# A hybrid decoder block: two segments of 256 tokens in place of segments of 128 and 384

## The chip, the cores and the metric

The kernel runs on one core of a Trainium2 chip. It is one program on that core's five engines: TensorE (PE in the profile, with its weight loads shown apart as PEld), VectorE (DVE), ScalarE (ACT), GpSimd (POOL) and SyncE (SP), which here only issues DMAs. The metric is the device time of one launch in microseconds (us); lower is better. The time before is 1791.47 us, the median of two runs (1790.25 and 1792.68).

## The reference

The input is 512 tokens of 1024 channels in float32. What is computed, cut to what matters:

```python
xn   = rmsnorm(h, mix_norm_w)
proj = xn @ w_in              # pool groups | q,k,v | z | beta | decay | gates
y_a  = pool_mixer(xa, ...) @ w_pool_up         # causal windows 2, 4, 8, 16
y_b  = deltanet_branch(qkv, z, ...) @ w_dn_up  # 8 heads, conv of 4, chunked scan
h    = h + (sigmoid(gate_a) * y_a + sigmoid(gate_b) * y_b) @ w_mix_out
h    = h + peer_ffn(rmsnorm(h, ffn_norm_w), ...)
out  = rmsnorm(h, final_norm_w)

def peer_ffn(x, w_query, keys_1, keys_2, expert_down, expert_up):
    # per token and head: top 16 of 128 keys on either side, top 16 of the
    # 256 sums, softmax: 8 * 16 = 128 of 16384 experts with a gate each
    act = gelu(x . expert_down[e])
    return sum over e of gate[e] * act * expert_up[e]
```

The convolution, the pools and the scan run causally over the tokens. The last layer, the experts (peer_ffn), has 16384 rows of 1024 floats in each of its two tables.

## The kernel before

**Blocks and segments.** The 512 tokens are four blocks of 128. The front of the block, from the first normalization to the choice of the experts, is written as `segment(t0, T)`: for T tokens from t0 it loads each weight matrix once, tile by tile (0.5 MB per tile, tag `wraw`, five buffers), and multiplies all T tokens with it. `SEGMENTS` (L59) says which segments there are. Before, the first holds block 0 (128 tokens) and the second blocks 1, 2 and 3 (384 tokens). The state of the scan and the last few tokens of the convolution and of the pools are handed from one segment to the next.

**Two ways to multiply.** A segment of fewer than 256 tokens is exact: its 60 tiles of `win` and `wdn` (52 and 8) are multiplied in plain float32. From 256 tokens on the weights are split: ScalarE writes the high part of each half tile (`whi`), VectorE the rest (`wlo`), and three products of high and low parts replace the exact one, with activations split in the same way (`xwide`). `wpu`, `wmo` and `wq` are never split.

```python
exact = T < 256                                                     # L718
def wload(ap, n, exact=False):                                      # L642
    ...
    for q in range(2):
        hi, lo = whi([P, 512], F32R), wlo([P, 512], F32R)
        split(raw[:, q * 512:(q + 1) * 512], (hi, lo))
```

**Two ways to do the experts.** Blocks 0 and 1 are gathered. `select` (L958) finds the 128 experts of each of the block's tokens, and `retrieve` (L1030) fetches for each of the 128 slots one row per token from the table `down`, has VectorE take its dot product (`rows<-rows,xbuf`), applies the gelu and the gate in groups of 16, then fetches the row of `up` and has VectorE add it to the token (`hbuf<-rows,keep,hbuf`). That is 256 gathers of 0.5 MB per block, 512 in all, issued by GpSimd into four buffers, tag `rows`. Blocks 2 and 3 (the last TB = 256 tokens) are dense: `dense` (L1062) goes over the whole tables, 128 tiles of each, computes all activations and multiplies them with gates that are zero for experts not chosen. The first 28 activation tiles (`PLAIN`) are plain float32 and the others split. `gates_of_experts` builds the gates on VectorE, ScalarE and TensorE.

**The tag keep.** The small tiles of a gathered block, its indices, gates, `act` and `co`, each take one of the six units of the tag `keep` (L533), and so does the gate tile of a dense block between its `select` and its transposition.

**What sets the order.** All instructions are first recorded, then a planner (`Order.schedule`) puts them into one fixed order per engine. Among the instructions that are ready by its own costs it takes the one with the smallest virtual time: 0 for the first segment, 10 for the second, 149 for a gather, from 150 on for the dense experts (`VTS`, `FETCH`, `MOVE`); a gathered block's `select` in a segment that also has dense blocks is put at 120 (`LATE`). On the chip each engine then runs its list strictly in that order, so an instruction that waits holds up all that stand behind it on its engine. Every instruction of the profile has line 495, the one that emits the plan; groups are told apart by tile names.

Of the kernel before, what the change touches and what calls it, by code (L numbers as in the profile page):

```python
# [55 lines left out]
PARTVT = 10.0  # L56
LATE = 120.0
PLAIN = RUN
SEGMENTS = ((0, 128), (128, 384))  # L59
TB = 256  # L60
TMAX = 384

# [451 lines left out]
def block_kernel(ctx: ExitStack, tc: tile.TileContext, x, win, wbd, poolw, wpu, wdn, wmo, wq, down, up, downt,  # L514
# [819 lines left out]

    for k, (t0, T) in enumerate(SEGMENTS):
        nc.vt = VTS[k]
# [56 lines left out]
```

## Time and profile before

| | |
|---|---|
| median of the runs | 1791.47 us |
| profiled execution, device time | 1788.57 us |
| its span, first to last instruction | 1786.8 us |
| busy in that span | TensorE 94%, VectorE 86%, ScalarE 52%, GpSimd 42% |
| read from HBM | 505 MB, 284 GB/s over the span |
| mean granted TensorE clock | 0.977 of full speed |

The profile is one execution. A busy share is a mean over the whole span, in which stages with different limits follow one another: the first segment (to about 240 us), the second with the gathers of block 0 beside it (to about 925 us), and the dense experts with the rest of the gathers (to the end). The device time lies 1.8 us over the span, and the median another 2.9 us over that.

### The profile page before, as it was taken

How to read it: one execution, taken by the hardware profiler on the slowest of the kernel's cores; microseconds unless marked ns; L12 is line 12 of the kernel's file. 1: busy time of each engine (PE TensorE's matmuls, PEld its weight loads, DVE VectorE, ACT ScalarE, POOL GpSimd, SP SyncE). 2: the span in 40 equal slices, each digit the busy share in tenths (PEclk: the TensorE clock that was granted, in tenths of full speed). 3: DMA queues.
4: the chain of work that ended last, by engine and by line, in shares of the span. 5: the costliest groups of instructions: out<-in, count | busy, mean ns of one | idle time of the engine just before them, and what ended most of it. 6: DMA issues, size and time to landing. Idle time of an engine off the chain costs nothing.

```text
span 1786.8 us, 34168 instructions
## 1 busy us (share of the span) xinstructions
PE 1677.1 (94%) x12186; PEld 1455.6 (81%) x12186; DVE 1542.0 (86%) x3873; ACT 922.9 (52%) x2271; POOL 755.4 (42%) x598
## 2 busy tenths in 40 slices
PE   7999999899999999998999999899999999999992
PEld 7999899889899898498787765677777768988892
DVE  6622499988998788699999999999999999999996
ACT  6642248845734342221139946666667665555552
POOL 0000015555466653543328743545445534333334
PEclk9999999899999999999999999999999999999996
DMA  7437858567687899897767798889999999999996
GB/s 262 154 125 253 278 191 281 188 225 259 205 265 255 304 349 328 312 315 240 236 214 255 240 355 310 313 320 331 348 348 330 348 334 379 345 341 345 340 353 226
DMA packets 144746, 509.36 MB, mean 285 GB/s; under 512 B 16960, under 2 KB 21184, under 8 KB 144576
## 3 DMA queue, kind: packets, MB, share of 16 engines
q0 software_dynamic: 73728, 268.47, 43.6%
q1 hardware_dynamic: 70848, 238.72, 37.6%
q8 instruction: 95, 1.56, 0.3%
q14 instruction: 75, 0.61, 0.1%
HBM read 505.02 MB, written 2.10 MB: 284 GB/s over the span
## 4 chain that ended last, share of the span: by engine, by line
PE 42%; DVE 26%; issue 13%; DMA 10%; POOL 6%; ACT 3%; SPq 0%; POOLq 0%; DVEq 0%; ACTq 0%
PE bank L495 42%; DMA rows<-in_up_dram,keep 7%; DVE quad L495 5%; POOL rows L495 5%; DVE rows L495 4%; DVE scr L495 4%; DVE hbuf L495 4%; DVE wlo L495 4%; DMA rows<-in_down_dram,keep 2%; DVE sel L495 2%; ACT scr L495 1%; DVE xwide L495 1%; ACT L495 1%; ACT quad L495 1%; ACT whi L495 0%
## 5 line engine op out<-in xcount | busy, mean ns | idle before, releaser
L495 PE MATMUL bank<-xwide,whi 128*128 128x256 f32 (+1 forms) x2560 | 575.6, 310 | 1.1 <-ACT whi L495 1.0
L495 POOL DMA_INDIRECT rows<-in_up_dram,keep x256 | 366.0, 1430 | 367.5 <-DVE hbuf L495 170.9
L495 POOL DMA_INDIRECT rows<-in_down_dram,keep x256 | 318.0, 1242 | 431.2 <-DVE keep L495 282.1
L495 ACT CAST whi<-wraw 128x512 fp32r<-128x512 f32 x512 | 315.3, 619 | 294.4 <-PE bank L495 247.8
L495 PEld LDWEIGHTS bank<-xwide,whi 128*128 128x128 f32 x2560 | 432.4, 192 | 9.1 <-ACT whi L495 2.8
L495 PE MATMUL bank<-xwide,wlo 128*128 128x256 f32 (+1 forms) x1280 | 396.9, 310 | 7.1 <-DVE wlo L495 6.9
L495 DVE SCALAR_TENSOR_TENSOR hbuf<-rows,keep,hbuf 128x1024 f32<-128x1024 f32 x256 | 328.6, 1284 | 42.3 <-DMA rows<-in_up_dram,keep 41.7
L495 DVE TENSOR_TENSOR wlo<-wraw,whi 128x512 fp32r<-128x512 f32 x512 | 352.8, 704 | 13.0 <-ACT whi L495 9.4
L495 DVE CUSTOM_DVE_ANT_0 rows<-rows,xbuf 128x1024 f32<-128x1024 f32 x256 | 318.1, 1246 | 23.9 <-DMA rows<-in_down_dram,keep 22.7
L495 PEld LDWEIGHTS bank<-xwide,wlo 128*128 128x128 f32 x1280 | 245.1, 192 | 16.8 <-DVE wlo L495 12.0
L495 PE MATMUL bank<-whi,xwide 128*128 128x512 f32 x768 | 242.6, 397 | 4.1 <-ACT xwide L495 2.6
L495 PE MATMUL bank<-pair,wraw 128*128 128x128 f32 (+1 forms) x1600 | 217.8, 289 | 1.6 <-DVE xwide L495 0.8
L495 PEld LDWEIGHTS bank<-pair,wraw 128*128 128x128 f32 x1600 | 198.2, 196 | 9.2 <-DVE xwide L495 1.1
L495 PE MATMUL bank<-quad,wraw 128*128 128x256 f32 x704 | 172.1, 389 | 0.0
L495 PEld LDWEIGHTS bank<-whi,xwide 128*128 128x128 f32 x768 | 139.0, 189 | 35.1 <-ACT xwide L495 4.1
L495 PE MATMUL bank<-wlo,xwide 128*128 128x512 f32 x384 | 150.3, 394 | 9.3 <-DVE wlo L495 9.1
L495 ACT ACTIVATE scr<-c,c 128x128 bf16<-128x128 bf16 x384 | 139.6, 445 | 23.1 <-PE bank L495 23.0
L495 PEld LDWEIGHTS bank<-quad,wraw 128*128 128x128 f32 x704 | 127.2, 191 | 15.5 <-issue 0.8
L495 PE MATMUL bank<-wraw,quad 128*128 128x512 f32 x256 | 120.9, 610 | 2.0 <-DVE quad L495 2.0
L495 PEld LDWEIGHTS <-scr 128*128 128x128 bf16 x2304 | 72.3, 97 | 48.3 <-issue 27.7
L495 PEld LDWEIGHTS bank<-wlo,xwide 128*128 128x128 f32 x384 | 71.9, 188 | 30.1 <-DVE wlo L495 15.0
L495 ACT COPY quad<-bank 128x512 f32<-128x512 f32 (+2 forms) x119 | 55.4, 474 | 74.7 <-PE bank L495 62.9
(156 smaller groups left out, 2126.2 us busy)
## 6 DMA issues: line engine op xcount, KB each, us to landing
wraw<-in_downt_dram SPq DMA_DIRECT2D x128, 512.0 KB
wraw<-in_up_dram SPq DMA_DIRECT2D x128, 512.0 KB
wraw<-in_win_dram SPq DMA_DIRECT2D x104, 512.0 KB
wraw<-in_wq_dram SPq DMA_DIRECT2D x32, 512.0 KB
wraw<-in_wdn_dram SPq DMA_DIRECT2D x16, 512.0 KB
wraw<-in_wmo_dram SPq DMA_DIRECT2D x16, 512.0 KB
wraw<-in_wpu_dram SPq DMA_DIRECT2D x8, 512.0 KB
rows<-in_down_dram,keep POOLq DMA_INDIRECT x256
```

What stands on the lines that cost most here:

```text
L495: ins = getattr(getattr(self.nc, eng), meth)(*(real(a) for a in args), **{k: real(a) for k, a in kw.items()})
```

## The change

One line of numbers is changed. The first segment then holds blocks 0 and 1, both gathered, and the second blocks 2 and 3, both dense. As neither is shorter than 256 tokens, neither is exact, and all tiles of `win` and `wdn` are split in both.

```diff
-SEGMENTS = ((0, 128), (128, 384))
+SEGMENTS = ((0, 256), (256, 256))
```

The planner makes a new order from this. Two places matter below. The first is GpSimd's list. `scr<-scr` are its additions in the convolution (128x256 or 128x384) and the pools (widths a little over the segment's); `small` are small powers; `rows<-in_down_dram,keep` is a gather. Before, from the pools of the first segment on:

```order
L495 TENSOR_TENSOR scr<-scr 128x137
L495 TENSOR_TENSOR scr<-scr 128x129
L495 TENSOR_TENSOR small<-small,c_82 128x1
L495 DMA rows<-in_down_dram,keep 128x1024
L495 TENSOR_TENSOR scr<-scr 128x384
L495 DMA rows<-in_down_dram,keep 128x1024 x3
```

The same place of the list now:

```order
L495 TENSOR_TENSOR scr<-scr 128x256 x14
L495 TENSOR_TENSOR small<-small,c_82 128x4
L495 TENSOR_TENSOR scr<-scr 128x256 x2
L495 TENSOR_TENSOR small<-small,c_82 128x4
L495 TENSOR_TENSOR scr<-scr 128x256 x8
L495 TENSOR_TENSOR small<-small,c_82 128x4 x2
L495 TENSOR_TENSOR scr<-scr 128x271 x2
...
L495 TENSOR_TENSOR scr<-scr 128x257
L495 TENSOR_TENSOR small<-small,c_82 128x1 x2
L495 DMA rows<-in_down_dram,keep 128x1024 x4
```

The first gather still stands behind the whole first segment, which now has two blocks; on VectorE the choice of experts for both blocks stands ahead of the first gathered row.

The second place is VectorE's list where the dense blocks have chosen their experts and their gates are written (`keep<-sel,small`; `c_105` are the dense blocks' gates in the form that the gate building reads). `ISA rows,keep<-rows,xbuf` is the dot product with a gathered row of `down`, `ISA keep` reads its sum, `hbuf<-rows,keep,hbuf` adds a gathered row of `up`. Before:

```order
L495 RECIPROCAL small<-small 128x8
L495 ISA rows,keep<-rows,xbuf 128x1024
L495 ISA keep 128x1
...
L495 SCALAR_TENSOR_TENSOR hbuf<-rows,keep,hbuf 128x1024
L495 TENSOR_TENSOR keep<-sel,small 128x128
L495 TENSOR_TENSOR keep<-small,keep 128x16
L495 TENSOR_TENSOR keep<-sel,small 128x128
L495 CAST c_105<-sel 128x128
```

And now (left out are 11 more pairs of ISA rows ahead of the first sum, and between the x15 row and the gate 32 more pairs and 16 more sums):

```order
L495 RECIPROCAL small<-small 128x8
L495 TENSOR_TENSOR scr<-c_85,c_105 128x2x96 x2
L495 ISA rows,keep<-rows,xbuf 128x1024
L495 ISA keep 128x1
...
L495 SCALAR_TENSOR_TENSOR hbuf<-rows,keep,hbuf 128x1024
L495 TENSOR_TENSOR keep<-small,keep 128x16
L495 SCALAR_TENSOR_TENSOR hbuf<-rows,keep,hbuf 128x1024 x15
...
L495 TENSOR_TENSOR keep<-sel,small 128x128
L495 SCALAR_TENSOR_TENSOR hbuf<-rows,keep,hbuf 128x1024
L495 CAST c_105<-sel 128x128
```

In both orders the dense gates stand behind all 128 dot products and 96 or 97 of the sums of block 0, 224 gathered rows, give or take one. Before, 221 gathered rows stand ahead of the last top-16 search of the dense blocks; now 148 do, and the other 76 stand between it and the gates, with next to nothing else among them.

## Rows read from the trace of the kernel before

**Rows 1.** Page, busy time of each engine, and chain that ended last.

```profile
PE 1677.1 (94%) x12186; PEld 1455.6 (81%) x12186; DVE 1542.0 (86%) x3873; ACT 922.9 (52%) x2271; POOL 755.4 (42%) x598
...
PE 42%; DVE 26%; issue 13%; DMA 10%; POOL 6%; ACT 3%; SPq 0%; POOLq 0%; DVEq 0%; ACTq 0%
```

**Rows 2.** Windows: stretch, length, busy PE, PEld, DVE, ACT, POOL, clock, DMA share, GB/s.

```profile
0.00:240.50 240.50, 223.77 (x1854) 214.66 (x1855) 111.75 (x488) 102.71 (x284) 10.36 (x40) 0.99 0.65 219
0.00:270.00 270.00, 252.72 (x2056) 241.63 (x2057) 140.40 (x609) 118.04 (x313) 17.28 (x46) 0.99 0.63 211
...
270.00:925.00 655.00, 627.19 (x3822) 565.86 (x3821) 589.23 (x1536) 285.37 (x633) 328.57 (x262) 0.97 0.77 264
925.00:1030.00 105.00, 97.83 (x1117) 79.47 (x1116) 102.62 (x297) 92.35 (x308) 76.63 (x32) 1.00 0.77 257
1030.00:1775.00 745.00, 699.31 (x5197) 568.66 (x5195) 705.28 (x1430) 426.01 (x1017) 331.40 (x259) 0.98 0.93 336
```

**Rows 3.** Timeline: last key scores of the first segment, first gathered row, first dense gate.

```profile
240.29 0.39 PE L495 MATMUL bank<-sel,scr 128*128 128x128 f32 x2
...
270.32 1.21 DVE L495 CUSTOM_DVE_ANT_0 rows<-rows,xbuf 128x1024 f32<-128x1024 f32 x1
...
926.50 0.28 DVE L495 TENSOR_TENSOR keep<-sel,small 128x128 f32<-128x128 f32 x1
```

**Rows 4.** Windows, VectorE on tile rows alone: stretch, length, busy (instructions), clock, DMA, GB/s.

```profile
270.00:925.00 655.00, 285.75 (x224) 0.97 0.77 264
...
704.00:745.00 41.00, 21.83 (x18) 1.00 0.96 353
1758.00:1775.70 17.70, 11.58 (x10) 0.54 0.84 293
```

**Rows 5.** VectorE's waits from 270 to 925: us in total, times, longest.

```profile
DVE hbuf L495 <- DMA rows<-in_up_dram,keep: 28.8, 23, 3.1
DVE rows L495 <- DMA rows<-in_down_dram,keep: 16.8, 16, 3.0
```

**Rows 6.** Chain in order of time (start, us, what), at two runs of bare gathers.

```profile
735.96 7.46 DMA rows<-in_up_dram,keep
...
1760.96 5.26 DMA rows<-in_up_dram,keep
```

**Rows 7.** TensorE's timeline (start, us): exact tiles, split at 384, at 256.

```profile
144.10 42.55 PE L495 MATMUL bank<-pair,wraw 128*128 128x128 f32 x376
...
601.70 0.33 PE L495 MATMUL bank<-xwide,wlo 128*128 128x384 f32 x1
...
602.22 0.33 PE L495 MATMUL bank<-xwide,wlo 128*128 128x384 f32 x1
...
1552.36 0.28 PE L495 MATMUL bank<-xwide,wlo 128*128 128x256 f32 x1
...
1552.72 0.28 PE L495 MATMUL bank<-xwide,wlo 128*128 128x256 f32 x1
```

**Rows 8.** TensorE's timeline: wmo in the first segment; plain float32 at 256.

```profile
186.48 13.90 PE L495 MATMUL bank<-wraw,pair 128*128 128x512 f32 x32
...
857.84 17.86 PE L495 MATMUL bank<-quad,wraw 128*128 128x256 f32 x82
```

**Rows 9.** Groups by line and shape: the two halves of a split.

```profile
L495 DVE TENSOR_TENSOR wlo<-wraw,whi 128x512 fp32r<-128x512 f32 x512 | 352.8, 704 | 13.0 <-ACT whi L495 9.4 <-ACT scr L495 0.6
...
L495 ACT CAST whi<-wraw 128x512 fp32r<-128x512 f32 x512 | 315.3, 619 | 294.4 <-PE bank L495 247.8 <-ACT xwide L495 11.2 <-issue 6.7
```

**Rows 10.** VectorE's timeline: three low halves in a row, and what follows.

```profile
1596.70 1.89 DVE L495 TENSOR_TENSOR wlo<-wraw,whi 128x512 fp32r<-128x512 f32 x3
1598.51 1.28 DVE L495 SCALAR_TENSOR_TENSOR hbuf<-rows,keep,hbuf 128x1024 f32<-128x1024 f32 x1
```

**Rows 11.** Windows, VectorE on tile wlo alone, columns as in Rows 4.

```profile
270.00:925.00 655.00, 79.76 (x109) 0.97 0.77 264
```

## The prediction

> **What bounds the kernel now.** I read the page's busy times first: TensorE 94% and VectorE 86% of the span, and a chain that ended last with TensorE on 42% and VectorE on 26% of it [rows 1]. Neither number says which of the two a change would hit, so I went by stages with the windows [rows 2]. The reader should see four of them. Up to 270 us VectorE is busy for only 140 us and TensorE for 253: the first segment is TensorE's. From 270, when the first gathered row is used, to 925, just before the first dense gate [rows 3], TensorE has 627 of 655 us and VectorE 589. From 925 to 1030 the rest of block 0's rows and the first dense gates fill VectorE (103 of 105). From 1030 on, the gathers of block 1 and the dense tiles run side by side, with VectorE at 705 and TensorE at 699 of 745 us and the DMA engines at 0.93. So after 270 us both engines are nearly full, and the only real idle time of VectorE is the 130 us of the first stage.
>
> Two more views say what a gathered row costs. In the windows of tile rows, VectorE uses 224 of them from 270 to 925 [rows 4], 2.9 us apart, and its waits there are mostly for rows to land, 28.8 + 16.8 us [rows 5]. The rows are not always spread, though: from 704 to 745 they stand almost bare in VectorE's list, 18 of them in 41 us, 2.3 us each, though a row costs it 1.28 us (285.75 / 224); at the end, with nearly nothing else running, it is 10 in 17.7 us, 1.8 us each by the windows [rows 4]. The chain shows why: a row takes 5.3 to 7.5 us from its issue to VectorE [rows 6], and there are four buffers.
>
> **The change part by part.** I build the span from four pieces: the first gathered row, the rows beside the second segment, the bare rows ahead of the dense gates, and the rest.
>
> *TensorE's work.* An exact tile is 16 records; 376 of them take 42.55 us, 0.113 each, so 1.81 us a tile [rows 7]. A split tile is 24 matmuls: three take 0.52 us at 384 columns (4.16 us a tile) and 0.36 at 256 (2.88) [rows 7]. The 60 tiles cost 60 x (1.81 + 4.16) = 358 us before and 60 x 2 x 2.88 = 346 after. The unsplit matrices keep their total columns. TensorE gains 12 us in all, but the first segment loses: its 60 tiles go from 109 to 173 us (+64); the 256 records of wq go from 0.113 to 0.218 (17.86 / 82 [rows 8]), +27; wmo +14, its 13.90 us once more [rows 8]; wpu +7, 64 records by the same difference. The rest of the first segment (scan, transposes) is what is left of TensorE's 224 busy us up to 240 [rows 2]: 224 - 109 - 29 - 14 - 7, and less some 9 us that already belong to the second segment, about 56 us for one block, and once more for the second. Sum: +168. The last key scores, at 240 now [rows 3], move to 408. I add 15 us, as VectorE and ScalarE get two half tiles each per 2.88 us of TensorE on top of the convolution and can no longer stay ahead everywhere (bounds 0 to 40). From the last scores to the first gathered row are 30 us now [rows 3]; two blocks choose their experts in place of one, so 46 us (30 to 60). **First gathered row at about 470 us** (440 to 500), 200 later than now.
>
> *VectorE's work.* 120 more low halves: three in a row take 1598.51 - 1596.70 = 1.81 us [rows 10], so 0.60 us each, though the group shows 0.704 for one alone [rows 9]: +73 us (72 to 84). ScalarE gets 120 casts of 0.619 us, +74 us [rows 9], at nothing: it is busy for 923 of 1787 us [rows 1], and what it delays in the first segment is in the 15 us above. The other vector work has the same elements in about as many instructions, and is put at zero (-10 to +5). HBM traffic is the same, since each segment loads all weights in either case.
>
> *The rows beside the second segment.* 148 now stand ahead of the dense blocks' last search. VectorE's work until there: from 270 to 925 it has 589 us, of which 286 for rows [rows 4] and 80 for low halves [rows 11]; the other 223 were for three blocks, so 149 for two. 113 low halves at 0.73 (80 / 109) are 83, and 148 rows at 1.28 are 189: 421 us. TensorE's part is under 400 (173 + 55 + 28 + 14 + 112 for tiles, wq, wmo, wpu and scans), so VectorE decides. With waits for rows in proportion to today's (46 x 148 / 224 = 30): **450 us** (415 to 480).
>
> *The bare rows ahead of the dense gates.* 76 rows stand alone between the last search and the gates. Nothing can hide their latency, so they go at the pace of the bare run: 2.3 us each, **175 us**. The bounds are 1.8 (137 us, the run at the end, with nothing else on the DMA engines) and 2.9 (220 us, today's mean); I take the run at 704 since weights move beside it too. TensorE has 28 plain tiles to do there, 16 x 0.218 = 3.5 us each, 98 us, and then waits.
>
> The Trainium skill's page "DMA: Bandwidth & Descriptors" (section "Anatomy of one DMA — SWDGE (gpsimd) path") gives about 2.0 us plus the bytes by 436 GB/s for such a transfer, 3.2 us for 0.5 MB; the rows here take 5.3 to 7.5. By the page four buffers would turn around in about 5.4 us, 1.4 us a row, which would make the bare run some 107 us and the span about 1873; I go by the rows.
>
> *The rest.* From the gates on, both lists hold the same work, 288 rows and all the dense tiles, which take 1787 - 925 = 862 us now. The plain tiles, which TensorE now does beside the gate building, are done by then, but VectorE fills that stretch [rows 2], so I credit 15 us (0 to 40).
>
> Sum: 470 + 450 + 175 + 847 = 1942 us of span. The device time lies 1.8 us above the span and the median 2.9 above that, so **about 1945 us**, 8.6% slower. A measurement of this kernel tells about 2% from no change.
>
> **The rivals.**
> 1. *Only the work counts.* VectorE's extra 73 us come on top and the late gathers are caught up with, as other work fills the bare run: 1788 + 73 = 1860. For it: VectorE is nearly full after 270 us [rows 2]. Against it: its list is fixed and the rows stand alone there.
> 2. *Rows come as fast as four buffers allow without load.* With 1.4 to 1.8 us a row, 107 to 137 us, the span is 1875 to 1905.
> 3. *The first segment chokes.* If VectorE and ScalarE can't keep to 2.88 us a tile and the rows go at today's 2.9, then 500 + 480 + 220 + 850 = 2050.
> 4. *Not slower.* TensorE alone is the bound: it gains 12 us, VectorE's extra work falls into its 130 idle us, and the 98 us of plain tiles done during the wait come off the rest in full. With the lower bounds of the other pieces, 440 + 415 + 137 + 764 = 1756 us, and 1788 if only part of the 98 comes off. The rest is what decides: TensorE would have to be what holds it up. For it speaks 94% busy [rows 1]; against it, that VectorE is as full there [rows 2].
>
> That the change does less than it says is ruled out by the order: 512 rows, 632 low halves, and the two waits shown.
>
> **How the numbers follow.** Forecast 0.58, rival 1 0.15, rival 2 0.14, rival 3 0.08, rival 4 0.05. The range of the forecast alone, with its pieces mostly not all at one end, is 1890 to 2000. To hold 8 in 10 it takes in rival 2 and most of rival 1: 1855 to 2000. Faster by over 2% needs rival 4 at its far end, 0.01; within 2% the rest of it, 0.04; slower 0.95.
>
> **What would show it.** The first gathered row near 470 us and not before 430. VectorE under two thirds busy until then. A stretch of some 175 us, near 920 to 1095, in which GpSimd issues a row about every 2.3 us, VectorE waits for DMAs between them, and TensorE runs out of plain tiles, idles, and may be granted a lower clock. First dense gates near 1095 in place of 925, and about 850 us from there to the end. Split matmuls at 256 columns 0.12 us apart, VectorE's busy time near 1610. If the gates come on time and the end is late all the same, the pieces are wrong; if the stretch after the gates shrinks by far more than 15 us, TensorE was the bound there and rival 4 has the better mechanism.

## The result, and the profile after

The kernel after takes 1992.02 us (median of two runs, 1989.1 and 1994.94) where the kernel before took 1791.47: 1.1103 times as long, with an interval of 1.1057 to 1.1148, 200 us more. The prediction was 1945 us in a range of 1855 to 2000, so the time came out inside the range and 47 us above the forecast. The profiled execution took 1989.1 us, its span is 1987.3, and its mean granted clock is 0.929 (0.977 before).

The page of the kernel after, busy times and two of its rows of 40 slices:

```profile
PE 1704.6 (86%) x12426; PEld 1477.4 (74%) x12426; DVE 1626.9 (82%) x3978; ACT 990.7 (50%) x2414; POOL 738.7 (37%) x621
...
DVE  7656525389998987779866799999999999999996
...
PEclk9899989997999899989975599999999999999997
...
L495 DVE TENSOR_TENSOR wlo<-wraw,whi 128x512 fp32r<-128x512 f32 x632 | 435.4, 699 | 102.0 <-ACT whi L495 97.8
```

TensorE's work is nearly what it was [rows 1] and VectorE's grew by 85 us, but the span grew by 200. Two places in the slices stand out: VectorE is at two to seven tenths for its first eight slices, some 400 us (before, its idle first stage ended at 270 us [rows 2]), and at the slices of 7, 5 and 5 tenths of the clock, from 994 to 1143 us, TensorE is busy for 33 of 149 us.

The four pieces of the prediction are seen in the timeline of the kernel after, with the last key scores of the first segment, the first gathered row, and the first dense gate:

```profile
456.05 0.61 PE L495 MATMUL bank<-sel,scr 128*128 128x128 f32 x4
...
495.56 1.21 DVE L495 CUSTOM_DVE_ANT_0 rows<-rows,xbuf 128x1024 f32<-128x1024 f32 x1
...
1128.06 0.29 DVE L495 TENSOR_TENSOR keep<-sel,small 128x128 f32<-128x128 f32 x1 [0.34 <-ACT small L495]
```

In [rows 3] these stood at 240, 270 and 926. The windows of the kernel after between them, columns as in Rows 2 (975.30 is where the first of the bare rows starts):

```profile
0.00:456.50 456.50, 419.58 (x2926) 386.35 (x2926) 256.07 (x810) 232.13 (x541) 35.42 (x67) 0.96 0.36 119
0.00:495.50 495.50, 442.01 (x3062) 402.95 (x3063) 294.79 (x1028) 241.34 (x558) 40.70 (x72) 0.94 0.35 116
495.50:975.30 479.80, 435.12 (x2924) 394.03 (x2924) 423.69 (x1103) 225.21 (x517) 210.82 (x185) 0.95 0.79 270
975.30:1128.30 153.00, 44.35 (x202) 37.10 (x199) 95.61 (x125) 5.58 (x17) 92.62 (x75) 0.65 0.85 295
1128.30:1987.30 859.00, 783.14 (x6242) 643.34 (x6242) 812.77 (x1727) 518.62 (x1322) 394.56 (x290) 0.96 0.90 322
```

And VectorE on tile rows alone in two of them, columns as in Rows 4:

```profile
495.50:975.30 479.80, 187.12 (x148) 0.95 0.79 270
975.30:1128.30 153.00, 94.87 (x77) 0.65 0.85 295
```

148 rows stand beside the second segment, as the order said, and then 76 stand bare (the window's 77th is the sum that starts right behind the first gate), 2.0 us each. TensorE does 44 us of work in those 153. What VectorE waited for, beside the second segment (first two lines) and in the bare run (columns as in Rows 5):

```profile
DVE rows L495 <- DMA rows<-in_down_dram,keep: 11.3, 11, 2.3
DVE hbuf L495 <- DMA rows<-in_up_dram,keep: 10.8, 9, 2.4
...
DVE rows L495 <- DMA rows<-in_down_dram,keep: 33.9, 32, 3.4
DVE hbuf L495 <- DMA rows<-in_up_dram,keep: 22.6, 24, 2.2
```

The last two are all of its 57 idle us in the bare run: nothing hides the landing of a row there. From the first dense gate to the end it is 859 us, with VectorE busy for 813; before, nearly the same work took 862 with 812 (from 925 on, [rows 2] and [rows 1] less the stages ahead).

**VectorE's ledger.** The span is VectorE's busy time plus its idle time, and each piece can be read from the windows. Until the first row VectorE idles for 495.5 - 294.8 = 201 us (270 - 140 = 130 before, [rows 2]); beside the second segment for 56 (66 before); in the bare run for 57; after the gates for 46 (49 before). That is +71 - 10 + 57 - 3 = +115 us of idle time, and with 85 us more work it is the 200. The entries hang together, and the experiments ask which of them cause the rest.

### The profile page after: what moved, and what is told of

Read it like the earlier page. It is cut to its first block, busy times and chain, and to the rows that moved or that the text cites. A ratio compares the mean times of both kernels' runs of the same rounds, so it can differ in the third digit from the quotient of the medians.

```text
span 1987.3 us, 35056 instructions
## 1 busy us (share of the span) xinstructions
PE 1704.6 (86%) x12426; PEld 1477.4 (74%) x12426; DVE 1626.9 (82%) x3978; ACT 990.7 (50%) x2414; POOL 738.7 (37%) x621
## 4 chain that ended last, share of the span: by engine, by line
PE 41%; DVE 22%; issue 14%; DMA 12%; POOL 6%; ACT 5%; SPq 0%; POOLq 0%; DVEq 0%; ACTq 0%
PE bank L495 41%; DMA rows<-in_up_dram,keep 8%; POOL rows L495 5%; DVE scr L495 5%; DVE rows L495 4%; DMA rows<-in_down_dram,keep 4%; DVE quad L495 4%; DVE wlo L495 3%; DVE hbuf L495 3%; DVE sel L495 1%; ACT scr L495 1%; ACT whi L495 1%; ACT quad L495 1%; ACT L495 1%; DVE xwide L495 1%
## 5 line engine op out<-in xcount | busy, mean ns | idle before, releaser
L495 PE MATMUL bank<-xwide,whi 128*128 128x256 f32 x3520 | 701.4, 293 | 9.6 <-ACT whi L495 4.3
L495 PEld LDWEIGHTS bank<-xwide,whi 128*128 128x128 f32 x3520 | 575.0, 196 | 17.8 <-ACT whi L495 6.2
L495 ACT CAST whi<-wraw 128x512 fp32r<-128x512 f32 x632 | 388.9, 619 | 329.2 <-PE bank L495 276.0
L495 PE MATMUL bank<-xwide,wlo 128*128 128x256 f32 x1760 | 515.2, 293 | 24.6 <-DVE wlo L495 24.5
L495 DVE TENSOR_TENSOR wlo<-wraw,whi 128x512 fp32r<-128x512 f32 x632 | 435.4, 699 | 102.0 <-ACT whi L495 97.8
L495 PEld LDWEIGHTS bank<-xwide,wlo 128*128 128x128 f32 x1760 | 345.9, 197 | 34.2 <-DVE wlo L495 29.8
L495 POOL TENSOR_TENSOR scr<-scr 128x256 f32<-128x256 f32 (+3 forms) x66 | 58.4, 885 | 162.8 <-DVE scr L495 120.6
L495 POOL TENSOR_TENSOR small<-small,c 128x1 f32<-128x1 f32 (+1 forms) x20 | 20.8, 1038 | 228.8 <-DVE small L495 224.8
L495 PE MATMUL bank<-pair,wraw 128*128 128x256 f32 x384 | 93.9, 389 | 10.7 <-ACT scr L495 8.3
L495 PE MATMUL bank<-scr 128*128 128x48 bf16 (+1 forms) x2304 | 81.2, 184 | 24.0 <-DVE scr L495 21.2
```

The source lines that it names most:

```text
L495: ins = getattr(getattr(self.nc, eng), meth)(*(real(a) for a in args), **{k: real(a) for k, a in kw.items()})
```

## The experiments

Every time is a median of its own runs, set against the kernel before on the same chip (1791 to 1796 us); the ratio and its interval are to that. The intervals reach 3 to 11 us to either side, so a difference of about 10 us between two runs is not clear of zero. Base is the kernel after, unless it says otherwise.

**1. The dense gates don't wait for keep.** The gate tile of a dense block is written over its exponentials.

```diff
-        gate = keep([P, P])
+        gate = keep([P, P]) if slots is None else ex.rearrange("p h k -> p (h k)")
```

> The kernel after, with the gate tile of a dense block written over its exponentials in place of a unit of keep, so that it needn't wait for block 0's rows; in VectorE's list 148 gathered rows then stand ahead of the dense gates in place of 224. Theory (the wait for keep, paid in VectorE's idle time): VectorE is what the end hangs on, so of the 153 us bare run only VectorE's idle share comes back, 153 - 96 = 57 us; about 1935 us (1915 to 1955), dense gates near 980, TensorE without a long idle stretch. Rival A (the wait stands on the path as a whole, the 76 rows are done for nothing beside other work): 1992 - 153 = about 1840. Rival B (only the extra split work counts, the wait is made good later): 1980 to 2000.

1967.48 us, ratio 1.0967 (1.0904 to 1.103): 25 us less, between the theory and rival B. The gates came at 958 and 977 in place of 1128, as they should. The windows of this run from the second dense gate on:

```profile
977.00:1820.00 843.00, 815.46 (x6437) 670.48 (x6435) 813.14 (x1750) 523.73 (x1333) 415.61 (x295) 1.00 0.93 335
1820.00:1963.00 143.00, 0.00 (x0) 0.00 (x0) 93.10 (x98) 1.58 (x4) 82.04 (x70) 0.50 0.83 275
```

TensorE is done at 1820, and behind it stand 73 rows (VectorE on tile rows in the last window), 1.96 us each, with TensorE idle and at its lower level. The bare run wasn't removed, it moved to the end: with VectorE and TensorE both 96 to 97% busy beside the dense tiles there was no room for the rows there in this order. So the wait that I had predicted is real, and yet taking it away gives back little. That the cost lies in the rows' not being done earlier is a guess at this point; experiments 4 and 5 test it.

**2. The same edit to the kernel before.**

> The kernel before, with the same edit as the first run: the dense blocks' gate tiles in place. There 221 rows stand ahead of the dense blocks' last search anyway, so the gates move past next to no row. Theory: no change, 1791 (1780 to 1800). Rival (the edit itself is worth time, whatever the order of rows, since it takes a wait away in both kernels): as many us as it gives the kernel after, 1735 or so.

1791.99 us, ratio 0.9994 (0.9973 to 1.0016). No change, as expected: the edit is worth something only where rows stand between the search and the gates.

**3. First segment exact.** The 120 low halves and 120 casts that the change added are gone, the segmentation stays.

```diff
-        exact = T < 256
+        exact = t0 == 0
```

> The kernel after, with the first segment of 256 tokens multiplied exactly, so that only the second one has split weights: 120 low halves and 120 casts fewer, as many as before, while its 60 tiles cost TensorE 16 x 0.22 = 3.5 us in place of 2.88. Theory (the first segment is TensorE's, and the extra low halves fall into VectorE's idle time there): nothing is won, and TensorE's 60 x 0.64 = 38 us put the first gathered row from 496 to about 530; about 2025 us (2005 to 2040). Rival A (the extra split work is what costs): 2.5 to 4% faster, 1992 - 75 = about 1917. Rival B (the first segment is held up by the two halves, not by TensorE): first row before 496 and 1960 to 1990.

1982.86 us, ratio 1.1057 (1.0998 to 1.1115): 9 us less, which the intervals don't tell from zero. VectorE's busy time fell by 92 us, from 1627 to 1534.9, and the time by some 9, so the extra low halves do fall into idle time, and rival A is out. That half of the theory holds, but its time and its mark are missed: the first row came at 484.5, not at 530, though the 60 tiles cost TensorE some 38 us more. The first segment was not TensorE's alone. Rival B had this, and its range and its mark are met. The windows of this run and its key scores' end:

```profile
0.00:445.00 445.00, 431.08 (x2377) 378.25 (x2378) 166.86 (x661) 152.53 (x407) 32.52 (x67) 0.98 0.38 122
```

```profile
444.79 0.38 PE L495 MATMUL bank<-sel,scr 128*128 128x128 f32 x2
```

TensorE is busy for 431 of 445 us here; in the kernel after it was 420 of 456 (the next two runs on this are 10 and 11).

**4. The late first row alone.** The kernel before, 128 and 384 tokens with all its work, and only the gathers of block 0 held back behind the convolution of the second segment (the list is made ahead of both; the second line stands in `gather`, the last two in `segment`, behind the convolution).

```diff
+    held = []
...
+            held.append(len(nc.ops))
...
+            if g and t0:
+                nc.ops[held[0]][1].add(len(nc.ops) - 1)
```

> The kernel before, 128 and 384 tokens, with block 0's gathers held back in the order until the convolution of the second segment is through (near 460 us in place of 270); nothing else is changed, no work is added. The order then has 154 or so rows ahead of the dense blocks' search and the rest bare ahead of the dense gates, as in the kernel after. Theory (the late first row is the main cost): the 76 rows that VectorE used from 270 to 495 are 100 us of its work that is done later, and the bare run adds up to 57 us of idle time: 1791 + 100 to 155, 1890 to 1945, 1920 taken. Rival A (the split work is the cost, late gathers are caught up with): 1790 to 1805. Rival B (the whole delay of 190 us is paid): 1980.

1904.23 us, ratio 1.0627 (1.0568 to 1.0686): 111 us more, as the theory said. The first row came at 448.66 (first line), and the windows of this run show the bare run of the kernel after, with no other part of the change in it:

```profile
448.66 1.22 DVE L495 CUSTOM_DVE_ANT_0 rows<-rows,xbuf 128x1024 f32<-128x1024 f32 x1
...
0.00:448.60 448.60, 429.65 (x3295) 415.51 (x3296) 240.16 (x844) 246.48 (x601) 46.66 (x71) 0.98 0.46 154
448.60:903.00 454.40, 435.80 (x2506) 383.14 (x2505) 397.40 (x1150) 146.34 (x330) 212.94 (x169) 0.98 0.80 275
903.00:1043.20 140.20, 28.65 (x146) 22.73 (x145) 94.89 (x158) 6.91 (x16) 81.58 (x68) 0.61 0.81 275
```

By the ledger, VectorE's idle time grows by 79 us ahead of the first row (448.6 - 240.2 = 208, 130 before) and by 34 behind it (115 to 149.6), while its work stays.

**5. Held back less far** (`if not g and t0`).

> The kernel before with block 0's gathers held back half as far, until the convolution of the second segment's first four heads is through (near 350 us in place of 270; held to 449 it took 1904 us, 113 more, with 68 rows bare at 2.06 us each). Some 26 rows then stand bare ahead of the dense gates. Theory (each us of delay leaves rows that are made up for only one after another, nothing absorbs them): 113 x 26 / 68 = 43 us more, about 1835 (1820 to 1850). Rival (the order has slack for a moderate delay and only a long one runs dry): 1790 to 1805.

1820.23 us, ratio 1.0143 (1.0087 to 1.0199): 25 us more, by the interval 16 to 36. The first row came at 311, earlier than I had meant:

```profile
311.38 2.02 DVE L495 CUSTOM_DVE_ANT_0 rows<-rows,xbuf 128x1024 f32<-128x1024 f32 x1
```

Per us of delay that is 24.6 / 41 = 0.60 (0.4 to 0.9), and in experiment 4 it is 111 / 178 = 0.62. The theory's count of bare rows came out (25, from 899 to 953.5 us), but not its price: 25 us for 25 rows here, 111 for 68 there. So the cost went with the delay and not with the bare rows, and the rival's slack is not seen, though one of up to some 15 us (an estimate from the interval) is not ruled out.

**6. Five row buffers** (and four weight buffers, `wraw`, to make room).

```diff
-    wraw = nc.tag("wraw", sb, D, 5)
+    wraw = nc.tag("wraw", sb, D, 4)
-    rows = nc.tag("rows", sb, D, 4)
+    rows = nc.tag("rows", sb, D, 5)
```

> The kernel after with five row buffers in place of four, and four weight buffers in place of five to make room. Theory (VectorE is what fills the time, four buffers cost only where rows stand bare): the 153 us bare run goes from 2.0 to about 1.6 us a row, and some of the 22 us of waits for rows beside the second segment go: 1940 to 1970, less whatever four weight buffers cost. Rival (the gathers' own pace is the bound: from the first row to the end all kernels so far take 2.84 to 2.96 us for each of 512 rows, 2.91 here): with five buffers that pace falls to about 2.5 until VectorE's 1333 us of work stop it, 1890 to 1920.

1958.91 us, ratio 1.0904 (1.0842 to 1.0966): 33 us less, within the theory's range. The bare run has fewer rows and each takes less time; VectorE on tile rows in this run:

```profile
975.00:1085.50 110.50, 77.77 (x62) 0.71 0.93 340
```

62 rows at 1.8 us in place of 76 at 2.0. From the first row (493.2) to the end of the span (1956.3) it is 2.86 us a row, where the rival had about 2.5: the steady 2.84 to 2.96 of the other kernels is not a limit that a fifth buffer lifts. The edit changes two numbers at once, and how much of the 33 us is the weight buffers' no run on this kernel tells (experiment 9 does so for experiment 8).

**7. The same two numbers in the kernel before.**

> The kernel before with five row buffers and four weight buffers. Theory (VectorE fills the time): it waits 64 us for rows in all, so at most 20 to 40 us come back, and four weight buffers may take as much: 1755 to 1800. Rival (the gathers' pace is the bound): 2.96 us a row falls to VectorE's limit of 1402 / 512 = 2.74, 1680 to 1710.

1801.8 us, ratio 1.0047 (1.002 to 1.0074): no gain, 2 us over the theory's range. The first row comes 9 us later here (279.5), and VectorE's idle time behind it is 117 us where it was 115. Where next to no row stands bare, the two numbers together buy nothing.

**8. Both: gates in place and five row buffers.**

> The kernel after with the dense gates in place (1967 us, which moved the bare run from the middle to the end: 73 rows in the last 143 us, 1.96 us each) and five row buffers, four weight buffers. In the order some 10 rows are left at the end in place of 75. Theory (the bare run is idle time of VectorE in whichever place it stands; with rows beside the dense tiles it goes): the 50 idle us of the tail come back in full, 1905 to 1925. Rival (VectorE and TensorE are both full beside the dense tiles, so rows moved there lengthen that stage by as much as the tail shrinks): 1950 to 1970.

1903.59 us, ratio 1.0607 (1.056 to 1.0654): 64 us less than experiment 1, 1 us below the theory's range. The windows of this run:

```profile
978.00:1880.00 902.00, 841.26 (x6434) 674.13 (x6432) 870.35 (x1806) 512.76 (x1331) 528.01 (x344) 0.99 0.94 343
1880.00:1901.90 21.90, 0.00 (x0) 0.00 (x0) 11.24 (x13) 2.95 (x6) 5.21 (x5) 0.56 0.58 215
```

The bare run is gone from the middle and from the end. The dense stage grew from 843 to 902 us with the rows that moved into it, which is the rival's reason, but the tail shrank by twice as much, from 143 to 22. After the first row VectorE now idles for 85 us, 52 less than in experiment 1 and less than the 115 of the kernel before, and still the kernel is 6% slower than that: what is left in the ledger is the idle time ahead of the first row and the extra low halves.

**9. The control: four row buffers again, four weight buffers.**

> The kernel after with the dense gates in place and four weight buffers, but four row buffers as it has: the fifth row buffer of the run at 1904 us taken away again. The order leaves 57 rows for the end, where it left 75 with five weight buffers and four row buffers (1967 us) and 10 with four and five (1904). Theory (each row that is left to stand bare costs VectorE's idle 0.7 us there, and the fifth row buffer is what keeps them from it): 1967 - 18 x 0.7 = about 1950 (1940 to 1960). Rival (the four weight buffers brought the gain, by spacing the dense tiles): 1900 to 1915.

1938.6 us, ratio 1.0813 (1.0794 to 1.0832). Between the two: of the 64 us the fifth row buffer gave 35, and one weight buffer fewer gave 29, more than the 18 rows that the order moved from the end can explain at 0.7 us each. Why fewer weight buffers help here stays open. In the kernel before they were never changed alone; together with the fifth row buffer (experiment 7) they gave nothing.

**10. High halves on VectorE** in the first segment, to relieve ScalarE.

```diff
-            w = wload(win[tl], KD, exact)
+            w = wload(win[tl], KD, exact, t0 == 0)
...
-        nc.scalar.copy(dst[0], src)
+        if early:
+            nc.vector.tensor_copy(dst[0], src)
+        else:
+            nc.scalar.copy(dst[0], src)
```

> The kernel after, with the high halves of the first segment's win tiles cast by VectorE, which idles there, in place of ScalarE; nothing else is changed. Theory (the first segment is held up by ScalarE, whose evictions of each product stand in one list with the casts: without the split the last scores came 11 us earlier although TensorE had 39 us more to do): last scores from 456 to 425 to 445, and at the 0.65 us per us that a later or earlier first row has cost so far, 1970 to 1985. Rival (it is held up by the halves' coming late, whichever engine makes them, or by VectorE): first row at 495 or later, 1990 to 2005.

1985.51 us, ratio 1.1066 (1.104 to 1.1091). The 7 us are not clear of zero, and the theory's mark is missed: the last scores came at 451, not at 425 to 445, though 104 casts had left ScalarE, and TensorE waited for ScalarE's evictions as long as before (15.9 us, 13.8 in the kernel after). The rival's mark is missed as well, by a first row at 490.9. The casts in ScalarE's list are not what holds the first segment up.

**11. Four buffers for each half of a split** in place of three, on the kernel of experiment 9.

```diff
-    whi = nc.tag("whi", sb, 512, 3)
-    wlo = nc.tag("wlo", sb, 512, 3)
+    whi = nc.tag("whi", sb, 512, 4)
+    wlo = nc.tag("wlo", sb, 512, 4)
```

> The run at 1939 us (dense gates in place, four weight buffers) with four buffers for the high and four for the low halves in place of three each. With three, the second half of the next tile can't be written before TensorE is through with the present one (ScalarE's casts waited 84 us for that up to 456 us in the kernel after). Theory (that is what holds the first segment up): last scores from 452 to 440 or earlier, and the time 1925 to 1932. Rival (TensorE loses its time there to evictions and to the low clock that follows its waits, whatever the halves do): last scores 448 to 456. In both the order leaves 63 rows for the end in place of 57, which costs some 4 us.

1931.36 us, ratio 1.0775 (1.0736 to 1.0813). The theory holds: last scores at 429 in place of 452. The timeline of this run, and then who waited for whom up to 440 us (us in total, times, longest):

```profile
429.04 0.50 PE L495 MATMUL bank<-sel,scr 128*128 128x128 f32 x3
...
468.81 1.21 DVE L495 CUSTOM_DVE_ANT_0 rows<-rows,xbuf 128x1024 f32<-128x1024 f32 x1
```

```profile
PE bank L495 <- ACT scr L495: 3.0, 4, 2.1
...
ACT whi L495 <- PE bank L495: 54.9, 65, 2.3
```

In experiment 9, up to 452 us, the same two waits were longer, and so they were in the kernel after, up to 456 (last two lines):

```profile
PE bank L495 <- ACT scr L495: 19.8, 16, 3.7
...
ACT whi L495 <- PE bank L495: 76.8, 76, 3.6
...
PE bank L495 <- ACT scr L495: 13.8, 10, 3.9
...
ACT whi L495 <- PE bank L495: 84.3, 70, 5.2
```

The windows up to the last scores, of experiment 9 and of this run, show that only TensorE's idle time has changed, 40 to 17 us:

```profile
0.00:452.40 452.40, 412.45 (x2910) 379.61 (x2911) 253.57 (x808) 228.79 (x541) 38.54 (x67) 0.97 0.36 119
...
0.00:429.50 429.50, 412.80 (x2924) 385.71 (x2925) 250.83 (x806) 227.40 (x543) 36.22 (x67) 0.96 0.37 127
```

With two halves to a tile, three buffers hold one tile and a half. My reading is that while TensorE works on one tile only half of the next can be made, and that a single late eviction then stops it. That the number of buffers matters is shown; this step from it to the waits is not. The time fell by 7 us, which the intervals don't tell from zero; at 0.6 a us the 23 us of first row are 14, and some 4 are lost to the six more rows that this order leaves for the end.

**12. Experiment 8 with the first segment exact.**

> The kernel at 1904 us (dense gates in place, five row and four weight buffers) with the first segment of 256 tokens multiplied exactly: 85 us less work for VectorE. Theory (the first segment's low halves fall into time in which VectorE idles, so only the first row's 11 us count, at 0.65 each): 1892 to 1898. Rival (with the bare run gone VectorE is full and its extra work shows now): 40 to 85 us less, 1820 to 1865.

1891.88 us, ratio 1.0523 (1.0476 to 1.057): 12 us less than experiment 8 for 92 us less work on VectorE (1614.9 to 1522.7), with the first row 10 us earlier (483.6). As expected, even with the bare run gone. It is the best 256/256 that I ran. No run beat the kernel before.

## Why the prediction held, step by step

**The first gathered row: 470 forecast, 495.6 measured.** The mechanism was right, the term was sized too low. TensorE's extra work was put at 168 us and the coupling at 15 (0 to 40), so last scores at 423; they came at 456. The coupling was the mis-sized part: 48 us in place of 15, and past its bound of 40. It has two halves in the trace: TensorE idles for 37 us up to there in place of 17, and it is busy for 420 us where 392 were counted. The timeline of TensorE in the kernel after, in the stretch where each tile is followed by eight matmuls of `wpu`:

```profile
263.62 0.41 PE L495 MATMUL bank<-xwide,wlo 128*128 128x256 f32 x1
...
264.26 0.42 PE L495 MATMUL bank<-xwide,wlo 128*128 128x256 f32 x1
...
268.07 3.57 PE L495 MATMUL bank<-pair,wraw 128*128 128x256 f32 x8 [2.40 <-ACT scr L495]
...
272.06 0.28 PE L495 MATMUL bank<-xwide,wlo 128*128 128x256 f32 x1
...
272.41 0.28 PE L495 MATMUL bank<-xwide,wlo 128*128 128x256 f32 x1
...
275.60 1.99 PE L495 MATMUL bank<-pair,wraw 128*128 128x256 f32 x8 [0.99 <-ACT scr L495]
```

From one wlo to the next there are three matmuls: 0.64 us at the first place, 0.35 at the second, and the eight matmuls take 3.57 and 1.99. The pitch of 0.12 that I took from [rows 7] does not hold around these waits, where TensorE ran at the lower of its two levels (granted clock 0.51 from 260 to 265 us, 1.00 from 272 to 276). Experiment 11 parts the two halves: with four buffers the idle time is back at 17 us, so that half comes from too few buffers. TensorE is still busy for 413 us there, so the other half, 21 to 28 us, does not. The granted clock up to the last scores is 0.96 or 0.97 in all three runs and 0.99 before [rows 2], so some of it is time at the lower level; the rest was not taken apart. The step from last scores to first row was 39.5 us, 46 forecast.

**Rows beside the second segment: 450 forecast, 480 measured,** the upper bound. VectorE's work was right (421 forecast, 424 measured). Its waits for rows are 22 us and not more than the 30 I allowed; what I had left out is that it also waits for TensorE and ScalarE, for most of the other 34 us. I had TensorE at under 400 us there and it is busy for 435, among other things with eight plain tiles that I had counted in the bare run, so "VectorE decides" was only half true.

**Bare rows: 175 forecast, 153 measured.** The count of 76 was exact, and 2.0 us a row lie between my row (2.3) and the run at the end (1.8, [rows 4]). The Trainium skill's page "DMA: Bandwidth & Descriptors" (section "Anatomy of one DMA — SWDGE (gpsimd) path") gives a fit that comes to an estimated 3.2 us for such a transfer, and the prediction had estimated 1.4 us a row from it. This trace does not agree: the rows took a median of 6.0 us from issue to landing in the bare run, and the bare runs of 57 to 76 rows on four buffers that were read took 1.87 to 2.06 us a row; the measurement decides.

**The rest: 847 forecast, 859 measured.** The credit of 15 us for the plain tiles done in the meantime came to 3. I had all 28 plain tiles, 98 us, done in the bare run. Of their 448 records (16 a tile), 188 ran there; TensorE's list then has the first dense gate's transposition, for which it waits 108.8 us, and the last 128 stand behind that. The groups of plain float32 matmuls follow, two of the kernel before (270 to 925 us, and behind) and three of the kernel after (beside the second segment, in the bare run, and behind the gates), and then the transposition. In the first group of either kernel 256 records are `wq`.

```profile
L495 PE MATMUL bank<-quad,wraw 128*128 128x256 f32 x516 | 123.1, 387 | 0.0
L495 PE MATMUL bank<-quad,wraw 128*128 128x256 f32 x190 | 49.5, 393 | 0.0
...
L495 PE MATMUL bank<-quad,wraw 128*128 128x256 f32 x390 | 94.7, 392 | 0.0
L495 PE MATMUL bank<-quad,wraw 128*128 128x256 f32 x188 | 41.3, 381 | 0.0
L495 PE MATMUL bank<-quad,wraw 128*128 128x256 f32 x128 | 34.7, 407 | 0.0
...
1128.40 0.48 PE L495 MATMUL bank<-c,keep 128*128 128x128 f32 x1 [108.76 <-DVE keep L495]
```

In the kernel before only 12 of the 28 tiles stood behind the gates, and now it is 8. So TensorE's work in this stretch fell by 14 us (797 to 783) and not by 98, and VectorE's stayed at 812 to 813. The credit was wrong in its premise, and its small size kept the miss small. Rival 4 had the same premise. Its time of 1756 to 1788 is refuted by the result, but whether TensorE or VectorE holds that stretch up no run here decides: its sign, a stretch much shorter than 847, could not show.

The sum of the misses is +26 + 30 - 22 + 12 = 46 us, which is the 45 between 1942 and the span of 1987.3. That the time stayed 8 us inside the range is in part luck: the first two pieces came out at the top of their bounds, and the bare rows, faster than I had them, took back 22 of the 56 us. TensorE's busy time over the whole span, which I had falling by 12 us, rose by 27 [rows 1], at a mean granted clock of 0.929 in place of 0.977.

**Low halves and casts.** VectorE's busy time rose by 85 us (73 forecast), as the 120 halves stand one by one between their casts: their group costs 435.4 us in place of 352.8 [rows 9], 0.69 for each one more and not 0.60. I counted the added halves inside the TensorE-bound stretch as free, and experiments 3 and 12 show that they nearly are: 92 us less work, 9 and 12 us less time, with a first row 10 to 11 us earlier.

**The rivals.** Rival 1 (only the work counts, late gathers are caught up with) falls by experiments 4 and 5: with no work added, the delay alone costs 0.6 us per us. Rival 2's pace of 1.4 to 1.8 was reached only at its upper end, and only by five buffers in a bare run of this length. Rival 3 came nearer than its chance of 0.08: its first row at 500, its 480 beside the second segment and its 850 behind the gates lie within 9 us of what was measured, and only its 2.9 us for a bare row was wrong.

**Where the reading of the forecast was too simple.** I wrote of the bare run as if the wait for the dense gates made it. Experiment 1 takes that wait away and gets back 25 of 153 us, as the rows then stand bare at the end. The bare run is the place where rows that came too late are made up for, and only with a better interleaving (experiment 8) does its idle time go. The main cause is the late first row: 225 us at the 0.6 of experiments 4 and 5 are some 135 to 140 of the 200 us. This is an estimate, as it carries a price from the kernel before, measured for delays of up to 178 us, over to another order. The remainder was not taken apart by a run of its own. The ledger says where it lies: experiment 4 has VectorE busy for 240 us until its first row at 449, and experiment 3, which has the change's segments without its extra halves, for 206 until 484.5. So the new order has less of VectorE's other work to do ahead of the late row, and the extra low halves fill part of the gap without shortening anything.

## What to carry to other kernels

When one engine carries a stream of work to the end, read its idle time ahead of the stream's first item before anything else: a change that starts the stream later can cost in proportion, here 0.6 us per us at delays of 41 and 178 us. A wait that stands on the path may still be worth little when it is removed, if the work that filled the wait only moves to another place; here the stage into which the rows would have had to move was 96 to 97% busy on both engines, and that is a thing to look at beforehand. Count a buffer in items of use: three half-tile buffers were one tile and a half, and with two whole tiles the first segment was done 23 us earlier. And count where each piece of work stands in an engine's list: of the plain tiles that I had in the bare run, more than half stood ahead of it or behind it.

## What the runs showed of the hardware

Bare gathers of 128 rows of 4 KB went at 2.0 us each with four buffers (295 GB/s in that window, DMA share 0.85) and at 1.8 with five (340 GB/s, 0.93), though VectorE needs 1.28. With four buffers it was much the same in the middle (2.0 and, in experiment 4, 2.06) and at the end (1.96 in experiment 1, 1.87 in experiment 9, 1.92 in experiment 11); the ten rows at the end of the kernel before went at 1.8.

TensorE's granted clock from 240 to 300 us was 0.91 in the kernel after, where TensorE was busy for 49.4 of the 60 us and waited 7.4 us for evictions, 2.4 at most. In experiment 3, where it never waited there, it was 1.00. But it was 0.97 in experiment 9, with 49.2 us busy and the same 7.4 us of waits, and 1.00 in experiment 10, with 52.3. So the same waits went with more time at the lower level in one run and with less in another; what decides was not tested.
